# Later modulation sums and the second parts of the weight pieces on VectorE alone

## The chip, the cores and the metric

The program runs on one core of a Trainium2 chip. The metric is the device time of one execution in microseconds (us). TensorE multiplies (PE in the profile; PEld is its weight load), VectorE (DVE), ScalarE (ACT) and GpSimd (POOL) work element by element, and SyncE (SP) issues most of the loads. Each engine takes its instructions in order and waits for others by semaphores.

## The reference, cut to what matters

A network of two layers runs over 256 latent tokens of width 2048, with 256 context tokens beside them in layer 0. Everything is float32.

```python
for l in range(DEPTH):
    sh1, sc1, g1, sh2, sc2, g2 = split(silu(c) @ ada_w[l] + ada_b[l], 6)   # the modulation
    h = modulate(x_lat, norm_mix[l], sh1, sc1)
    y = even_mixer(h, hc, ...) if l % 2 == 0 else shortconv_mixer(h, ...)
    x_lat = x_lat + g1 * y
    x_lat = x_lat + g2 * swiglu(modulate(x_lat, norm_ffn[l], sh2, sc2), w_gate, w_up, w_down)
return rmsnorm(x_lat, final_norm)
```

`even_mixer` is a gated delta rule in chunks (8 heads, both directions) beside a neighbourhood attention (8 heads). The modulation is a vector times a matrix of 2048 x 12288 per layer, with nothing to reuse: its cost is the load of that matrix and one multiply-add per element.

## The kernel before, in words

**Weights.** A float32 product is made from two parts of each factor. A weight piece is 128 x 1024 numbers: `load_w` loads it (tile `raw`, 512 KB), ScalarE rounds it into `whi` (L170, called in `split_w`), and `wlo`, the rest, is `raw - whi`. For the pieces of the even mixer's input projection (112 of them, `LO_CUT = 576`) VectorE makes the first 576 columns of `wlo` (L238) and GpSimd the other 448 (L240). For all later pieces (688, `LO_CUT2 = 1024`) VectorE makes the whole. TensorE multiplies hi by hi, hi by lo and lo by hi: in `fm_stream` at L304 and L308 (256 columns a matmul), in `tm_stream` at L279, L280, L282 and, for a stream's last two steps, bank by bank at L288 to L290 (512 columns). A step of `tm_stream` over two token tiles is 12 matmuls for one piece. Pieces lie in 3 buffers of `whi` and `wlo` in the even mixer and in 4 after it; `raw` has 4 and then 6.

**The modulation.** The first sixth and second sixth of layer 0 are made on TensorE at the start (L481). All others, which the change calls the later sums, are made by `ada_job` block by block: 12 blocks of 512 columns (the even mixer and its output projection) and 14 of 1024 (layer 0's feed-forward, the odd mixer, layer 1's feed-forward). A block loads 16 tiles `araw`, one for each 128 rows, scales each by a column of `cT` and adds them up. In 12 of the 16 steps VectorE does both in one instruction, into `acc` (L335). In the steps k = 1, 5, 9, 13 ScalarE scales (L330 into `acc2` for k = 1, L332 in place for the others) and GpSimd adds into `acc2` (L333). At the end GpSimd adds `acc2` to `acc` (L337), the sum is split into `ah` and `al` (ScalarE L173, VectorE L174; blocks of 512 skip this) and TensorE adds up its partitions (L350 or L342). `araw` has 2 buffers for blocks of 1024 columns and 3 for those of 512; `acc` has one.

**What sets the order.** A `Pump` doles out steps of these blocks between the steps of the weight streams. The order on each engine is then laid out by the framework's scheduler, which models the time of every instruction. So an instruction that changes its engine or its length moves others on all engines.

**Stages in the profiled execution** (us from the start of the span): start with layer 0's first modulation to 146; the even mixer's first projections and the delta rule's matrices to 410; the rest of the even mixer, the attention and the output projection, all woven together, to 980; layer 0's feed-forward, gate and up to 1500 and down to 1755; the odd mixer to 2170; layer 1's feed-forward to the end, with modulation steps up to 2480.

Of the kernel before, what the change touches and what calls it, by code (L numbers as in the profile page):

```python
# [23 lines left out]
F32 = mybir.dt.float32  # L24
F32R = mybir.dt.float32r
AF = mybir.ActivationFunctionType
OP = mybir.AluOpType
# [5 lines left out]
FK = FH // 128  # L33
EPS = 1e-6
HD = 128
LO_CUT = 576
LO_CUT2 = 1024
RAW = 4
G2 = 4
XDT = 2  # L40
# [15 lines left out]
RAW2 = 6  # L56
SP2 = 4
# [49 lines left out]
def body(tc, x, c, ctx, c_ctx, ada_w, ada_b, norm_mix, norm_ffn, ffn_w_gate, ffn_w_up, ffn_w_down,  # L107
# [37 lines left out]
    wp = dict(pool=pool("weights", stack=wstk), raw=RAW, split=3, cut=LO_CUT)  # L145
    mm = pool("mm", bufs=4, space=PSUM)
    sm = pool("sm", bufs=2, space=PSUM)
    dram = pool("scratch", space=bass.MemoryType.DRAM)
# [79 lines left out]
            o += w  # L228
        return raw.rearrange("p k n -> p (k n)")

    def split_w(raw, cut):

        cut = wp["cut"] if cut is None else cut
        hi = wp["pool"].tile([128, 1024], F32R, name="whi", tag="whi", bufs=wp["split"])
        lo = wp["pool"].tile([128, 1024], F32R, name="wlo", tag="wlo", bufs=wp["split"])
        acopy(hi, raw)
        if cut:
            DVE.tensor_tensor(lo[:, 0:cut], raw[:, 0:cut], hi[:, 0:cut], op=OP.subtract)  # L238
        if cut < 1024:
            POOL.tensor_tensor(lo[:, cut:], raw[:, cut:], hi[:, cut:], op=OP.subtract)  # L240
        return hi, lo

    def w_steps(segs, ks, cut):

        W = sum(s[2] for s in segs)
        nk = 1024 // W
        for g in range(0, len(ks), nk):
            assert ks[g + nk - 1] == ks[g] + nk - 1
            hi, lo = split_w(load_w(segs, ks[g], nk), cut)
            for j in range(nk):  # L250
                yield ks[g] + j, hi[:, j * W:(j + 1) * W], lo[:, j * W:(j + 1) * W]

# [9 lines left out]
            else:  # L262
                yield i, []

    def tm_stream(segs, ks, lhs, toks, evac, cut=None):

        W = sum(s[2] for s in segs)
        nb = W // 512
        ps = [[None] * nb for _ in toks]
        for i, group in grouped(((k, (hi, lo) + lhs(k)) for k, hi, lo in w_steps(segs, ks, cut)), len(ks)):  # L270
            first, last = i == 0, i == len(ks) - 1
            if len(group) == 1 and not last:
                hi, lo, lh, ll = group[0]
                for ti, t in enumerate(toks):
                    a, b = lh(t), ll(t)
                    for n in range(nb):
                        if first:
                            ps[ti][n] = mmt()
                        PE.matmul(ps[ti][n], a, hi[:, n * 512:(n + 1) * 512], start=first, stop=False)  # L279
                        PE.matmul(ps[ti][n], a, lo[:, n * 512:(n + 1) * 512], start=False, stop=False)  # L280
                    for n in range(nb):
                        PE.matmul(ps[ti][n], b, hi[:, n * 512:(n + 1) * 512], start=False, stop=last)  # L282
            else:
                for ti, t in enumerate(toks):
                    for n in range(nb if group else 0):
                        for hi, lo, lh, ll in group:
                            c_ = slice(n * 512, (n + 1) * 512)
                            PE.matmul(ps[ti][n], lh(t), hi[:, c_], start=False, stop=False)  # L288
                            PE.matmul(ps[ti][n], lh(t), lo[:, c_], start=False, stop=False)  # L289
                            PE.matmul(ps[ti][n], ll(t), hi[:, c_], start=False, stop=hi is group[-1][0])  # L290
                        evac(ti, n, ps[ti][n])
            yield

    def fm_stream(segs, ks, ws, evac, cut=None):

        ps = [None] * 4
        for i, group in grouped(((k, (k, hi, lo)) for k, hi, lo in w_steps(segs, ks, cut)), len(ks)):
            for f in range(4):
                if i == 0:
                    ps[f] = mmt()  # L300
                for g, (k, hi, lo) in enumerate(group):
                    a, b = hi[:, f * 128:(f + 1) * 128], lo[:, f * 128:(f + 1) * 128]
                    if i == 0:
                        PE.matmul(ps[f][:, 0:len(ws) * 256], a, h0[:, 0:len(ws) * 256], start=True, stop=False)  # L304
                    for j, (wt, mv) in enumerate(((a, h_hi), (a, h_lo), (b, h_hi))):
                        for n, w in enumerate(ws):
                            if j or i:
                                PE.matmul(ps[f][:, n * 256:(n + 1) * 256], wt, mv(w, k), start=False,  # L308
                                          stop=i == len(ks) - 1 and g == len(group) - 1 and j == 2 and w == ws[-1])
                if i == len(ks) - 1:  # L310
                    evac(f, ps[f])
            yield


    def ada_job(pool_, l, seg, kind, gamma=None, width=1024, bufs=2):

        wr = ada_w[l].rearrange("(k p) n -> p k n", p=128)
        nf = width // 128
        for blk in range(D // width):
            c0 = seg * D + blk * width  # L320
            acc = pool_.tile([128, width], F32, name="acc", tag="acc", bufs=1)
            acc2 = pool_.tile([128, width], F32, name="acc2", tag="acc2", bufs=1)
            POOL.memset(acc, 0.0)
            SP.dma_start(acc[0:1, :], ada_b[l:l + 1, c0:c0 + width])
            for k in range(KT):
                raw = pool_.tile([128, width], F32, name="araw", tag="araw", bufs=bufs)
                SP.dma_start(raw, wr[:, k, c0:c0 + width])
                col = cT[:, k:k + 1]
                if k == 1:
                    ACT.activation(acc2, raw, AF.Copy, scale=col)  # L330
                elif k % 4 == 1:
                    ACT.activation(raw, raw, AF.Copy, scale=col)  # L332
                    POOL.tensor_tensor(acc2, raw, acc2, op=OP.add)  # L333
                else:
                    DVE.scalar_tensor_tensor(acc, raw, col, acc, op0=OP.mult, op1=OP.add)  # L335
                yield
            POOL.tensor_tensor(acc, acc, acc2, op=OP.add)  # L337
            fs_ = slice(blk * nf, (blk + 1) * nf)
            p = smt()
            if width < 1024:  # L340
                for f in range(nf):
                    PE.matmul(p[:, f:f + 1], acc[:, f * 128:(f + 1) * 128], ones[:, 0:1], start=True, stop=True)  # L342
                pc = p
            else:
                ah = pool_.tile([128, width], F32R, name="ah", tag="ah", bufs=1)
                al = pool_.tile([128, width], F32R, name="al", tag="acc2", bufs=1)
                split(ah, al, acc, DVE)
                for f in range(nf):
                    for a in (ah, al):
                        PE.matmul(p[0:nf, 0:128], pick[:, nf - 1 - f:2 * nf - 1 - f], a[:, f * 128:(f + 1) * 128],  # L350
                                  start=f == 0 and a is ah, stop=f == nf - 1 and a is al)
                g = pool_.tile([16, 128], F32, name="grow", tag="grow", bufs=1)[0:nf]
                acopy(g, p[0:nf, 0:128])
                if kind == "row":
                    ACT.dma_start(row_d[l, seg][fs_], g)
                    continue
                pc = smt()
                transpose(pc[:, 0:nf], g)
            if kind == "sc":
                DVE.scalar_tensor_tensor(scc[l, seg - 1][:, fs_], pc[:, 0:nf], 1.0, gamma[:, fs_], op0=OP.add, op1=OP.mult)  # L360
            else:
                DVE.tensor_copy((shc if kind == "sh" else gcol)[l, seg][:, fs_], pc[:, 0:nf])
        if kind == "row" and width < 1024:
            p = smt()
            transpose(p[0:16, 0:128], gcol[l, seg])
            g = pool_.tile([16, 128], F32, name="grow", tag="grow", bufs=1)
            DVE.tensor_copy(g, p[0:16, 0:128])
            SP.dma_start(row_d[l, seg], g)
# [97 lines left out]
    ks = list(range(KT))  # L466
# [667 lines left out]
    nastk.close()  # L1134
    hlstk.close()
    wstk.close()
    wp.update(pool=pool("weights2"), raw=RAW2, split=SP2, cut=LO_CUT2)
    small.append(pool("sm2", bufs=2, space=PSUM))


# [259 lines left out]
```

## Time and profile before

| | us |
|---|---|
| median of 3 runs | 2939.82 (2938.19 to 2940.96) |
| the profiled execution | 2944.36 |
| its span, first to last instruction | 2942.5 |
| TensorE busy in it | 2757.0 |
| VectorE busy | 1896.3 |
| ScalarE busy | 1335.1 |
| GpSimd busy | 587.1 |

The span is 1.9 us shorter than the execution's own time, which is 4.5 us above the median of the three timed runs. Busy time is the union of an engine's instructions; TensorE's matmuls overlap one another, so its rows give a longer time for a matmul than the distance from one to the next. The mean granted clock of TensorE is 0.981 of full speed. A measurement of this kernel can tell a difference of about 0.2% (6 us) from none.

### The profile page before, as it was taken

What the parts mean: (1) busy time and instruction counts of PE and PEld (TensorE: products, weight loads), DVE (VectorE), ACT (ScalarE), POOL (GpSimd) and SP (SyncE); (2) the same over time, 40 slices, a digit from 0 to 9 for tenths busy, and PEclk for the clock granted to TensorE, in tenths of its full rate; (3) what the DMA queues carried; (4) which work ended last, traced back from release to release, by engine and by line L of the source; (5) the groups of instructions that cost most, each with busy time, mean ns of one, the idle gap of its engine ahead of it and who ended that gap; (6) DMA issues with size and microseconds to landing.
All of it is one profiled execution on the core that took longest, in us unless ns stands there. A gap on an engine that the chain in (4) does not pass through costs nothing. (4 is left out here: it accounts for less than half of the span.)

```text
span 2942.5 us, 40694 instructions
## 1 busy us (share of the span) xinstructions
PE 2757.0 (94%) x15113; PEld 2292.6 (78%) x15113; DVE 1896.3 (64%) x2409; ACT 1335.1 (45%) x1822; POOL 587.1 (20%) x431
## 2 busy tenths in 40 slices
PE   5898998989899999999999999999999999999997
PEld 3688988878777778878877777777777888888886
DVE  3378766845566777666667867777767446445675
ACT  3245544333354444444445555453544444444554
POOL 1147535336322111110111101111101001000010
PEclk9999999999999999999999999999999999999999
DMA  9954567777767688877878766878568667656653
GB/s 344 297 156 115 159 196 242 240 225 222 218 191 245 236 290 287 301 265 260 274 252 274 261 198 239 296 259 301 196 193 294 194 186 257 187 186 217 191 193 122
DMA packets 284929, 680.80 MB, mean 231 GB/s; under 512 B 57273, under 2 KB 97313, under 8 KB 283323
## 3 DMA queue, kind: packets, MB, share of 16 engines
q1 hardware_dynamic: 262148, 652.48, 67.5%
q10 hardware_dynamic: 22583, 25.73, 2.9%
q8 instruction: 118, 1.93, 0.3%
q14 instruction: 80, 0.66, 0.1%
HBM read 657.63 MB, written 20.48 MB: 230 GB/s over the span
## 5 line engine op out<-in xcount | busy, mean ns | idle before, releaser
L238 DVE TENSOR_TENSOR wlo<-raw,whi 128x1024 fp32r<-128x1024 f32 (+1 forms) x800 | 1009.2, 1274 | 490.1 <-ACT whi L170 476.8
L170 ACT ACTIVATE whi<-raw 128x1024 fp32r<-128x1024 f32 x800 | 835.7, 1055 | 634.3 <-PE mm L282 449.5
L335 DVE SCALAR_TENSOR_TENSOR acc<-araw,cT,acc 128x1024 f32<-128x1024 f32 (+1 forms) x312 | 357.5, 1146 | 292.7 <-DMA araw<-in_ada_w_dram 252.4
L280 PE MATMUL mm<-wlo,fhi 128*128 128x512 f32 x1232 | 478.8, 394 | 3.6 <-DVE wlo L238 3.3
L279 PE MATMUL mm<-whi,fhi 128*128 128x512 f32 x1232 | 476.4, 397 | 0.0
L282 PE MATMUL mm<-whi,flo 128*128 128x512 f32 x1232 | 394.1, 393 | 0.0
L333 POOL TENSOR_TENSOR acc<-araw,acc 128x1024 f32<-128x1024 f32 (+1 forms) x78 | 155.7, 1996 | 1118.0 <-ACT araw L332 632.3
L280 PEld LDWEIGHTS mm<-wlo,fhi 128*128 128x128 f32 x1232 | 232.9, 189 | 57.8 <-DVE wlo L238 8.4
L282 PEld LDWEIGHTS mm<-whi,flo 128*128 128x128 f32 x1232 | 232.2, 189 | 50.2
L279 PEld LDWEIGHTS mm<-whi,fhi 128*128 128x128 f32 x1232 | 233.1, 189 | 48.6 <-ACT sg L1262 0.4
L279 PE MATMUL mm<-whi,ahi 128*128 128x512 f32 x672 | 262.1, 395 | 3.8 <-ACT ahi L173 2.0
L280 PE MATMUL mm<-wlo,ahi 128*128 128x512 f32 x672 | 261.8, 393 | 0.3 <-DVE wlo L238 0.3
L240 POOL TENSOR_TENSOR wlo<-raw,whi 128x448 fp32r<-128x448 f32 x112 | 160.2, 1432 | 279.8 <-ACT whi L170 259.8
L282 PE MATMUL mm<-whi,alo 128*128 128x512 f32 x672 | 211.5, 395 | 2.1 <-DVE alo L174 1.7
L332 ACT ACTIVATE araw<-araw,cT 128x1024 f32<-128x1024 f32 (+1 forms) x78 | 74.4, 954 | 301.0 <-DMA araw<-in_ada_w_dram 256.8
L308 PE MATMUL mm<-hllo,whi 128*128 128x256 f32 x640 | 184.6, 291 | 0.0
L308 PE MATMUL mm<-hlhi,wlo 128*128 128x256 f32 x600 | 172.1, 291 | 4.5 <-DVE wlo L238 4.5
L308 PE MATMUL mm<-hlhi,whi 128*128 128x256 f32 x600 | 170.2, 293 | 1.2 <-DVE hlhi L506 1.2
L1159 POOL TENSOR_TENSOR xs<-rtmp,xs 128x512 f32<-128x512 f32 x24 | 35.4, 1496 | 631.4 <-DVE rtmp L1157 631.4
L279 PEld LDWEIGHTS mm<-whi,ahi 128*128 128x128 f32 x672 | 126.8, 189 | 32.2 <-ACT ahi L173 2.8
L282 PEld LDWEIGHTS mm<-whi,alo 128*128 128x128 f32 x672 | 126.2, 189 | 32.2 <-DVE alo L174 5.1
L280 PEld LDWEIGHTS mm<-wlo,ahi 128*128 128x128 f32 x672 | 126.7, 189 | 29.4 <-DVE wlo L238 1.9
(398 smaller groups left out, 4677.6 us busy)
## 6 DMA issues: line engine op xcount, KB each, us to landing
araw<-in_ada_w_dram SPq DMA_DIRECT2D x288, 512.0 KB
raw<-in_ffn_w_down_dram SPq DMA_DIRECT2D x176, 512.0 KB
raw<-in_ffn_w_gate_dram SPq DMA_DIRECT2D x160, 512.0 KB
raw<-in_ffn_w_up_dram SPq DMA_DIRECT2D x160, 512.0 KB
raw<-in_ev_w_in_dram SPq DMA_DIRECT2D x112, 512.0 KB
araw<-in_ada_w_dram SPq DMA_DIRECT2D x192, 256.0 KB
raw<-in_od_w_in_dram SPq DMA_DIRECT2D x96, 512.0 KB
raw<-in_ev_w_out_dram SPq DMA_DIRECT2D x32, 512.0 KB
```

The costliest lines, as they stand in the source:

```text
L170: ACT.activation(dst, src, AF.Copy)
L238: DVE.tensor_tensor(lo[:, 0:cut], raw[:, 0:cut], hi[:, 0:cut], op=OP.subtract)
L240: POOL.tensor_tensor(lo[:, cut:], raw[:, cut:], hi[:, cut:], op=OP.subtract)
L279: PE.matmul(ps[ti][n], a, hi[:, n * 512:(n + 1) * 512], start=first, stop=False)
L280: PE.matmul(ps[ti][n], a, lo[:, n * 512:(n + 1) * 512], start=False, stop=False)
L282: PE.matmul(ps[ti][n], b, hi[:, n * 512:(n + 1) * 512], start=False, stop=last)
L308: PE.matmul(ps[f][:, n * 256:(n + 1) * 256], wt, mv(w, k), start=False, stop=i == len(ks) - 1 and g == len(group) - 1 and j == 2 and w == ...
L332: ACT.activation(raw, raw, AF.Copy, scale=col)
L333: POOL.tensor_tensor(acc2, raw, acc2, op=OP.add)
L335: DVE.scalar_tensor_tensor(acc, raw, col, acc, op0=OP.mult, op1=OP.add)
L1159: eng.tensor_tensor(v, tmp, v, op=OP.add)
```

## The change

The second part of a weight piece is always made by VectorE in one instruction of 1024 columns; the cuts are gone. In the modulation all 16 steps of a block are VectorE's multiply-add; ScalarE's scaling, GpSimd's adds and the final add are gone, and so is the tile `acc2`, whose place `al` had shared. GpSimd keeps its other work (zeroing `acc`, the delta rule's helpers, the residual adds).

```diff
@@ split_w
         acopy(hi, raw)
-        if cut:
-            DVE.tensor_tensor(lo[:, 0:cut], raw[:, 0:cut], hi[:, 0:cut], op=OP.subtract)
-        if cut < 1024:
-            POOL.tensor_tensor(lo[:, cut:], raw[:, cut:], hi[:, cut:], op=OP.subtract)
+        DVE.tensor_tensor(lo, raw, hi, op=OP.subtract)
         return hi, lo
@@ ada_job
             acc = pool_.tile([128, width], F32, name="acc", tag="acc", bufs=1)
-            acc2 = pool_.tile([128, width], F32, name="acc2", tag="acc2", bufs=1)
             POOL.memset(acc, 0.0)
...
                 SP.dma_start(raw, wr[:, k, c0:c0 + width])
-                col = cT[:, k:k + 1]
-                if k == 1:
-                    ACT.activation(acc2, raw, AF.Copy, scale=col)
-                elif k % 4 == 1:
-                    ACT.activation(raw, raw, AF.Copy, scale=col)
-                    POOL.tensor_tensor(acc2, raw, acc2, op=OP.add)
-                else:
-                    DVE.scalar_tensor_tensor(acc, raw, col, acc, op0=OP.mult, op1=OP.add)
+                DVE.scalar_tensor_tensor(acc, raw, cT[:, k:k + 1], acc, op0=OP.mult, op1=OP.add)
                 yield
-            POOL.tensor_tensor(acc, acc, acc2, op=OP.add)
...
-                al = pool_.tile([128, width], F32R, name="al", tag="acc2", bufs=1)
+                al = pool_.tile([128, width], F32R, name="al", tag="al", bufs=1)
```

In the changed program the lines have other numbers: the multiply-add is L321 (was L335), `wlo` L234 (was L238), `whi` L168 (was L170), the split of a sum L171 and L172 (were L173 and L174), the evacuations of layer 0's up stream L1251 (was L1266) and of the odd mixer L1309 (was L1324).

The order moves on every engine. Three places carry the prediction. The first is VectorE in layer 0's feed-forward, up to the evacuation `sg` of the second up stream; before, from the split `al` of a modulation block on:

```order
L174 TENSOR_TENSOR al<-acc,ah 128x1024
L238 TENSOR_TENSOR wlo<-raw,whi 128x1024
L335 SCALAR_TENSOR_TENSOR acc<-araw,cT,acc 128x1024
L238 TENSOR_TENSOR wlo<-raw,whi 128x1024 x3
L335 SCALAR_TENSOR_TENSOR acc<-araw,cT,acc 128x1024
L238 TENSOR_TENSOR wlo<-raw,whi 128x1024 x2
L335 SCALAR_TENSOR_TENSOR acc<-araw,cT,acc 128x1024
L238 TENSOR_TENSOR wlo<-raw,whi 128x1024 x2
L335 SCALAR_TENSOR_TENSOR acc<-araw,cT,acc 128x1024
L238 TENSOR_TENSOR wlo<-raw,whi 128x1024 x6
L1266 TENSOR_TENSOR sg<-mm,sg 128x512 x4
```

The same place of the changed program, up to the same evacuation:

```order
L234 TENSOR_TENSOR wlo<-raw,whi 128x1024 x2
L321 SCALAR_TENSOR_TENSOR acc<-araw,cT,acc 128x1024
L234 TENSOR_TENSOR wlo<-raw,whi 128x1024
L321 SCALAR_TENSOR_TENSOR acc<-araw,cT,acc 128x1024
L234 TENSOR_TENSOR wlo<-raw,whi 128x1024
L321 SCALAR_TENSOR_TENSOR acc<-araw,cT,acc 128x1024
L234 TENSOR_TENSOR wlo<-raw,whi 128x1024
L321 SCALAR_TENSOR_TENSOR acc<-araw,cT,acc 128x1024
L234 TENSOR_TENSOR wlo<-raw,whi 128x1024 x2
L321 SCALAR_TENSOR_TENSOR acc<-araw,cT,acc 128x1024
L234 TENSOR_TENSOR wlo<-raw,whi 128x1024
L1251 TENSOR_TENSOR sg<-mm,sg 128x512 x4
```

The multiply-adds stand closer together. Counted in the orders from a block's first multiply-add to its last, the 14 blocks of 1024 columns hold 15 to 19 weight pieces each in the changed program; before, six held 16 to 20 (layer 0's first two, three of the odd mixer's four and layer 1's first) and the other eight 25 to 31, one 70.

The second place is ScalarE there. Before, around the evacuation `sg` of a gate stream:

```order
L170 ACTIVATE whi<-raw 128x1024 x5
L332 ACTIVATE araw<-araw,cT 128x1024
L170 ACTIVATE whi<-raw 128x1024 x6
L332 ACTIVATE araw<-araw,cT 128x1024
L1262 ACTIVATE sg<-mm 128x512 x3
L170 ACTIVATE whi<-raw 128x1024
L1262 ACTIVATE sg<-mm 128x512
L170 ACTIVATE whi<-raw 128x1024 x3
L173 ACTIVATE ah<-acc 128x1024
```

And in the changed program:

```order
L168 ACTIVATE whi<-raw 128x1024 x7
L171 ACTIVATE ah<-acc 128x1024
L168 ACTIVATE whi<-raw 128x1024 x5
L1247 ACTIVATE sg<-mm 128x512 x3
L168 ACTIVATE whi<-raw 128x1024
L1247 ACTIVATE sg<-mm 128x512
L168 ACTIVATE whi<-raw 128x1024 x17
```

The scalings between the `whi` are gone, and with them the places where ScalarE could wait for an `araw` to land.

The third place is VectorE at the end of the odd mixer's first value stream, where `u_t` takes the sums out of PSUM. Before:

```order
L335 SCALAR_TENSOR_TENSOR acc<-araw,cT,acc 128x1024
L238 TENSOR_TENSOR wlo<-raw,whi 128x1024
L1324 TENSOR_TENSOR u_t<-mm,u_t 128x512 x4
L335 SCALAR_TENSOR_TENSOR acc<-araw,cT,acc 128x1024
L238 TENSOR_TENSOR wlo<-raw,whi 128x1024 x2
```

In the changed program:

```order
L321 SCALAR_TENSOR_TENSOR acc<-araw,cT,acc 128x1024
L234 TENSOR_TENSOR wlo<-raw,whi 128x1024
L1309 TENSOR_TENSOR u_t<-mm,u_t 128x512
L321 SCALAR_TENSOR_TENSOR acc<-araw,cT,acc 128x1024
L1309 TENSOR_TENSOR u_t<-mm,u_t 128x512 x2
L321 SCALAR_TENSOR_TENSOR acc<-araw,cT,acc 128x1024
L1309 TENSOR_TENSOR u_t<-mm,u_t 128x512
L234 TENSOR_TENSOR wlo<-raw,whi 128x1024 x2
```

Two multiply-adds now stand among the four evacuations. Over all streams from layer 0's feed-forward on six stand so, and one did before.

More of the change, by code (lines that the diff above doesn't have):

```diff
@@ L144, in body @@
     wstk = Stack()
-    wp = dict(pool=pool("weights", stack=wstk), raw=RAW, split=3, cut=LO_CUT)
+    wp = dict(pool=pool("weights", stack=wstk), raw=RAW, split=3)
     mm = pool("mm", bufs=4, space=PSUM)
@@ L229, in load_w, with split_w @@
         return raw.rearrange("p k n -> p (k n)")
-    def split_w(raw, cut):
-        cut = wp["cut"] if cut is None else cut
+    def split_w(raw):
         hi = wp["pool"].tile([128, 1024], F32R, name="whi", tag="whi", bufs=wp["split"])
@@ L263, in grouped, with tm_stream @@
                 yield i, []
[L265 removed]
+    def tm_stream(segs, ks, lhs, toks, evac):
         W = sum(s[2] for s in segs)
@@ L269, in tm_stream @@
         ps = [[None] * nb for _ in toks]
-        for i, group in grouped(((k, (hi, lo) + lhs(k)) for k, hi, lo in w_steps(segs, ks, cut)), len(ks)):
+        for i, group in grouped(((k, (hi, lo) + lhs(k)) for k, hi, lo in w_steps(segs, ks)), len(ks)):
             first, last = i == 0, i == len(ks) - 1
@@ L292, in tm_stream, with fm_stream @@
             yield
-    def fm_stream(segs, ks, ws, evac, cut=None):
+    def fm_stream(segs, ks, ws, evac):
         ps = [None] * 4
-        for i, group in grouped(((k, (k, hi, lo)) for k, hi, lo in w_steps(segs, ks, cut)), len(ks)):
+        for i, group in grouped(((k, (k, hi, lo)) for k, hi, lo in w_steps(segs, ks)), len(ks)):
             for f in range(4):
@@ L1136, in body @@
     wstk.close()
-    wp.update(pool=pool("weights2"), raw=RAW2, split=SP2, cut=LO_CUT2)
+    wp.update(pool=pool("weights2"), raw=RAW2, split=SP2)
     small.append(pool("sm2", bufs=2, space=PSUM))
```

6 lines of the change are left out of this document (2 added, 4 removed).

## The prediction

> **What bounds the kernel now.** I read the page first: busy time by engine.
>
> ```profile
> PE 2757.0 (94%) x15113; PEld 2292.6 (78%) x15113; DVE 1896.3 (64%) x2409; ACT 1335.1 (45%) x1822; POOL 587.1 (20%) x431
> ```
>
> TensorE sets the end. Its matmuls are the same before and after, so the change can only move TensorE's idle time. The windows view, cut at the stages, says where that is (window, its length, then busy us of PE, PEld, DVE, ACT, POOL, granted clock, DMA share, GB/s):
>
> ```profile
> 146.00:410.00 264.00, 243.29 (x1941) 239.31 (x1941) 211.94 (x364) 131.33 (x196) 142.60 (x136) 0.96 0.48 142
> 410.00:980.00 570.00, 517.61 (x3973) 448.04 (x3972) 356.47 (x593) 229.51 (x407) 221.67 (x181) 0.98 0.74 230
> 980.00:1500.00 520.00, 509.18 (x2308) 415.06 (x2309) 357.34 (x325) 245.94 (x277) 64.64 (x29) 0.99 0.79 274
> 1500.00:1755.00 255.00, 242.55 (x1066) 192.94 (x1066) 183.96 (x206) 134.62 (x195) 35.10 (x15) 0.99 0.73 245
> 1755.00:2170.00 415.00, 389.36 (x1748) 313.62 (x1746) 299.77 (x338) 191.25 (x245) 58.50 (x30) 0.98 0.74 251
> 2170.00:2480.00 310.00, 300.87 (x1339) 246.27 (x1340) 189.08 (x193) 143.01 (x164) 22.91 (x10) 0.98 0.70 229
> ```
>
> Length less PE busy is idle time: 20.7 and 52.4 us in the even mixer's two stages, 10.8, 12.5, 25.6 and 9.1 in the four with blocks of 1024 columns. Before 146 and after 2480 the change touches little. So at most 131 us are in play, and the table of waits says for whom TensorE waits. First from 980 to 2480 (us in total, times, longest):
>
> ```profile
> PE sm L189 <- DVE xc L1174: 18.3, 3, 6.3
> PE sm L189 <- DVE sg L1266: 7.3, 2, 4.4
> PE mm L279 <- DVE u_t L1324: 7.2, 2, 4.3
> PE mm L280 <- DVE wlo L238: 5.4, 10, 1.0
> PE sm L189 <- DVE sg L1278: 4.9, 1, 4.9
> PE mm L289 <- DVE wlo L238: 2.8, 4, 1.0
> PE mm L279 <- ACT ahi L173: 2.0, 2, 1.0
> PE mm L282 <- DVE alo L174: 1.7, 4, 0.6
> PE mm L290 <- DVE alo L174: 1.4, 1, 1.4
> ```
>
> Three kinds: the norms between layers (xc, 18.3, untouched), late second parts and splits (5.4 + 2.8 + 2.0 + 1.7 + 1.4 = 13.3), and evacuations at a stream's end that VectorE made late (7.3 + 7.2 + 4.9 = 19.4). In the even mixer, from the table for the whole run, those that name GpSimd, and the longest one of VectorE's and ScalarE's convolution chain:
>
> ```profile
> PE sm L189 <- ACT cv L562: 12.6, 8, 2.8
> ...
> PE sm L1092 <- POOL bq L1087: 2.7, 1, 2.7
> ...
> PE gd L772 <- POOL gm L768: 2.5, 4, 0.8
> ...
> PE gd L883 <- POOL acc L333: 2.3, 1, 2.3
> ...
> PE sm L342 <- POOL acc L337: 1.6, 2, 0.9
> ```
>
> **The change part by part: VectorE's load.** How long its instructions take undisturbed, from the timeline (start, us):
>
> ```profile
> 602.67 0.75 DVE L335 SCALAR_TENSOR_TENSOR acc<-araw,cT,acc 128x512 f32<-128x512 f32 x1 [3.42 <-DMA araw<-in_ada_w_dram]
> 603.34 0.75 DVE L238 TENSOR_TENSOR wlo<-raw,whi 128x576 fp32r<-128x576 f32 x1
> 1871.79 1.22 DVE L238 TENSOR_TENSOR wlo<-raw,whi 128x1024 fp32r<-128x1024 f32 x1
> 1872.93 1.28 DVE L335 SCALAR_TENSOR_TENSOR acc<-araw,cT,acc 128x1024 f32<-128x1024 f32 x1
> ```
>
> Added: 112 whole pieces in place of 576 columns, 112 x (1.22 - 0.75) = 53 us; 4 steps in each of 14 wide and 12 narrow blocks, 56 x 1.28 + 48 x 0.75 = 108 us. Together 161 us. Against it stands what GpSimd costs VectorE today. The group means are well above those times:
>
> ```profile
> L238 DVE TENSOR_TENSOR wlo<-raw,whi 128x1024 fp32r<-128x1024 f32 x688 | 892.7, 1311 | 398.7 <-ACT whi L170 394.4 <-DMA raw<-in_ffn_w_up_dram 2.8
> L335 DVE SCALAR_TENSOR_TENSOR acc<-araw,cT,acc 128x1024 f32<-128x1024 f32 x168 | 227.5, 1354 | 180.4 <-DMA araw<-in_ada_w_dram 160.9 <-DMA acc<-in_ada_b_dram 10.3 <-issue 8.7
> L335 DVE SCALAR_TENSOR_TENSOR acc<-araw,cT,acc 128x512 f32<-128x512 f32 x144 | 130.0, 903 | 112.3 <-DMA araw<-in_ada_w_dram 91.5 <-DMA acc<-in_ada_b_dram 8.9 <-issue 8.0
> L238 DVE TENSOR_TENSOR wlo<-raw,whi 128x576 fp32r<-128x576 f32 x112 | 116.5, 1042 | 91.5 <-ACT whi L170 82.4 <-issue 5.2 <-DMA nd<-n 3.6
> ```
>
> The excess is 688 x 0.09 + 168 x 0.07 + 144 x 0.15 + 112 x 0.29 = 62 + 12 + 22 + 32 = 128 us. One case in the timeline shows its cause, a piece of 1024 columns that starts in the middle of a GpSimd add and ends 1.1 us after it, 2.58 us in place of 1.22:
>
> ```profile
> 1203.44 2.41 POOL L333 TENSOR_TENSOR acc<-araw,acc 128x1024 f32<-128x1024 f32 x1 [15.23 <-ACT araw L332]
> 1204.34 2.58 DVE L238 TENSOR_TENSOR wlo<-raw,whi 128x1024 fp32r<-128x1024 f32 x1 [1.75 <-ACT whi L170]
> ```
>
> Most of this excess goes, since the GpSimd work that goes is 160.2 + 155.7 + 64.7 = 381 of its 587 us:
>
> ```profile
> L240 POOL TENSOR_TENSOR wlo<-raw,whi 128x448 fp32r<-128x448 f32 x112 | 160.2, 1432 | 279.8 <-ACT whi L170 259.8 <-DMA qTd<-qf 5.9 <-issue 4.8
> L333 POOL TENSOR_TENSOR acc<-araw,acc 128x1024 f32<-128x1024 f32 (+1 forms) x78 | 155.7, 1996 | 1118.0 <-ACT araw L332 632.3 <-ACT acc L330 466.8 <-DVE sg L1266 11.9
> L337 POOL TENSOR_TENSOR acc<-acc,acc 128x1024 f32<-128x1024 f32 (+1 forms) x26 | 64.7, 2490 | 118.0 <-issue 108.7 <-DVE acc L335 3.4 <-DMA raw<-in_ev_w_out_dram 2.8
> ```
>
> So VectorE's busy time stays within some 30 to 50 us of what it was: about 1930 to 1945 us. The Trainium skill, page SBUF — State Buffer, section Who interferes with whom, has a VectorE instruction with two inputs in SBUF and a reading GpSimd instruction shut each other out for a whole instruction; by that rule up to GpSimd's full 381 us could come back, while the rows show 128.
>
> **ScalarE and the loads.** ScalarE loses its scalings, and two kinds of wait in which it held up the `whi` queued behind (waits of ScalarE, then of VectorE):
>
> ```profile
> ACT araw L332 <- DMA araw<-in_ada_w_dram: 256.8, 62, 9.4
> ...
> ACT ah L173 <- POOL acc L337: 77.4, 14, 7.3
> ...
> ACT acc L330 <- POOL acc L337: 22.4, 6, 6.2
> ```
>
> ```profile
> DVE acc L335 <- DMA araw<-in_ada_w_dram: 252.4, 156, 5.1
> ```
>
> The second and third go. The first moves: 104 more multiply-adds wait for `araw` on VectorE. At its mean, 252.4 / 312 = 0.81 us, that is 84 us of blocking where ScalarE had 257; behind a blocked VectorE stand the `wlo` and evacuations that TensorE needs, covered by the pieces made ahead. SP's 416 loads of `araw` stay and stand closer together. GpSimd's queue keeps zeroing `acc`; the chain between blocks loses L337.
>
> **The sum**, made against the profiled execution of 2944.4 us (span 2942.5 and 1.9 around it), which lies 4.5 us above the median; I take the differences to the median. (a) Late second parts and splits, 13.3 us: the stretched pieces go, the closer multiply-adds bring some back; -3, between -13 (all gone) and +13 (as much again). (b) Six multiply-adds among the evacuations where one was: one costs at most 1.28 + 0.81 = 2.1 us of lateness, and half is hidden behind the other banks' last matmuls; +5, between 0 and +11. (c) The even mixer: the waits for L333 and L337 go (3.9), half of those for `bq` and `gm` (2.6), since GpSimd's queue before them empties, and a third of the convolution's 12.6 (my estimate; its multiply-adds meet L240 today); -10, between -25 (a third of the 73 us idle there) and +13 (as much again as the convolution waits, if longer pieces on VectorE delay the small steps). Sum -8: **2932 us**.
>
> **The rivals.** *Slower: the closer blocks outrun the loads.* A wide block is now 16 loads of `araw` and about 17 of weights, 33 x 0.524 MB in the time TensorE takes for 17 pieces of 12 matmuls. Two matmuls in the chain of work that ended last (start, us):
>
> ```profile
> 2107.72 0.46 PE mm L282 x2
> ```
>
> So a piece is 2.75 us, and 17.3 MB in 46.8 us would be 370 GB/s. The page's rates by slice:
>
> ```profile
> GB/s 344 297 156 115 159 196 242 240 225 222 218 191 245 236 290 287 301 265 260 274 252 274 261 198 239 296 259 301 196 193 294 194 186 257 187 186 217 191 193 122
> ```
>
> No slice went above 344, and 301 after the start. VectorE would stand at an `araw` while `wlo` and evacuations wait; the three pieces ahead (8.2 us) cover rates down to 17.3 MB in 55 us, 315 GB/s, and below that it decides. Its price is to be read from blocks that were as close before: the odd mixer's 25.6 us less its norm (6.1) over four blocks is 4.9 each, gate and up of layer 0 have (10.8 - 6.1) / 6 = 0.8. Seven blocks that were wide apart become close: 7 x 4.1 = 29, and with (c) 2940 + 29 - 10 = 2959 us. Against it: the gaps between blocks become longer, so the lead comes back.
>
> *No change.* VectorE's sum is near zero, TensorE is 94% busy, and what ScalarE no longer waits for VectorE does: 2940 us.
>
> *Slower: whole pieces come late for their first columns.* In the even mixer a piece's first 512 columns serve one step and the others the next; the first are ready after 0.75 us today and after 1.22 then. All exposed that is 53 us, a quarter 13: 2953 us. Against it: the split's second half takes GpSimd 1.43 us (L240), longer than the whole. The Trainium skill, page Perfetto Trace Analysis, section Optimizing Scalar/DVE Operations, advises breaking instructions up where an unsaturated engine makes others wait; by that rule this is the outcome, and L240's row speaks against it here.
>
> **How the numbers follow.** Forecast 0.44, close blocks 0.29, no change 0.22, late columns 0.05. A measurement tells 0.2% (5.9 us) from none, so faster 0.44, same 0.22, slower 0.34. The forecast's own range is 2908 (all of (c)) to 2934; the range of 8 in 10 takes in no change and most of the close blocks: 2908 to 2962.
>
> **What would show it.** Right: no L240, L333, L337; group means of `wlo` near 1.22 and of the multiply-add near 1.28 and 0.75; VectorE busy 1915 to 1960; ScalarE without L330 and L332; fewer waits of TensorE for GpSimd in 410 to 980. Wrong: more idle TensorE between 980 and 2480 than 58 us, with VectorE waiting for `araw` much over 340 us in all (the first rival); or idle time in the even mixer grown by VectorE's names.

## The result, and the profile after

The changed kernel takes 2881.91 us (median of 5 runs, 2877.6 to 2893.09), the kernel before beside it 2938.19 (5 runs, 2933.56 to 2940.96): a ratio of 0.9823, with an interval of 0.9804 to 0.9842. It is 1.8% faster, and faster than the lower end of the predicted range. The profiled execution took 2891.65 us (span 2889.6), 9.7 above its median; the one before took 2944.36.

From the page of the changed kernel: the span, the busy time by engine, and the rates by slice.

```profile
span 2889.6 us, 40293 instructions
...
PE 2747.0 (95%) x15113; PEld 2297.8 (80%) x15113; DVE 1896.9 (66%) x2513; ACT 1263.6 (44%) x1720; POOL 216.0 (7%) x215
...
GB/s 342 300 171 133 145 205 252 242 216 193 221 176 224 215 336 318 330 266 273 308 277 265 230 190 239 336 310 298 178 206 327 241 182 183 190 188 216 192 191 123
```

VectorE's busy time is what it was (1896.3 before), though it has 104 instructions more. GpSimd lost 371 us of work. The windows, cut at the same stages (window, length, busy us of PE, PEld, DVE, ACT, POOL, granted clock, DMA share, GB/s):

```profile
146.00:410.00 264.00, 249.50 (x2048) 246.29 (x2046) 204.61 (x373) 134.44 (x196) 79.08 (x88) 0.99 0.53 155
410.00:987.00 577.00, 521.52 (x3889) 451.27 (x3889) 362.29 (x632) 201.22 (x359) 81.76 (x79) 0.94 0.72 222
987.00:1497.00 510.00, 504.21 (x2305) 413.90 (x2306) 373.98 (x362) 225.24 (x255) 6.68 (x7) 0.99 0.83 293
1497.00:1746.00 249.00, 248.04 (x1119) 201.99 (x1117) 177.13 (x211) 136.84 (x195) 9.26 (x8) 1.00 0.71 233
1746.00:2125.00 379.00, 371.39 (x1698) 304.06 (x1698) 289.41 (x342) 170.41 (x219) 12.75 (x12) 0.99 0.79 269
2125.00:2430.00 305.00, 299.60 (x1349) 246.43 (x1349) 190.47 (x202) 136.97 (x159) 2.62 (x3) 0.99 0.72 235
```

The four stages with wide blocks (the last four rows) last 1443 us where they lasted 1500. TensorE's idle time in them (length less busy) is 5.8, 1.0, 7.6 and 5.4 us, 19.8 in all, where it was 58.0. Its busy time fell too, from 1442.0 to 1423.2, with the same matmuls: the granted clock reads 0.99, 1.00, 0.99, 0.99 where it read 0.99, 0.99, 0.98, 0.98. So 38 of the 57 us are idle time that went, and 19 are busy time, of which the clock accounts for a part. The even mixer (the first two rows) gave nothing back. What TensorE waits for in the four stages now, the longest of the table of waits (us, times, longest):

```profile
PE sm L187 <- DVE xc L1159: 18.0, 3, 6.4
PE mm L273 <- ACT u_t L168: 1.2, 1, 1.2
PE mm L274 <- DVE wlo L234: 1.0, 1, 1.0
PE mm L273 <- DVE u_t L1309: 0.3, 1, 0.3
```

The norms between layers are left. The late second parts and splits (13.3 us before) are down to 1.0, the late evacuations by VectorE (19.4) to 0.3. VectorE's groups, with shapes apart:

```profile
L234 DVE TENSOR_TENSOR wlo<-raw,whi 128x1024 fp32r<-128x1024 f32 x800 | 982.9, 1235 | 494.0 <-ACT whi L168 484.7 <-DMA araw<-in_ada_w_dram 6.9 <-PE mm L302 0.8
L321 DVE SCALAR_TENSOR_TENSOR acc<-araw,cT,acc 128x1024 f32<-128x1024 f32 x224 | 287.4, 1283 | 123.4 <-DMA araw<-in_ada_w_dram 115.1 <-DMA acc<-in_ada_b_dram 3.6 <-issue 1.5
L321 DVE SCALAR_TENSOR_TENSOR acc<-araw,cT,acc 128x512 f32<-128x512 f32 x192 | 149.8, 780 | 120.6 <-DMA araw<-in_ada_w_dram 107.3 <-DMA acc<-in_ada_b_dram 11.2
L172 DVE TENSOR_TENSOR alo<-prodT,ahi 128x256 fp32r<-128x256 f32 x176 | 79.5, 454 | 67.8 <-PE mm L276 62.8 <-ACT ahi L171 5.0
```

The means, 1.235, 1.283 and 0.780 us, are close to the undisturbed 1.22, 1.28 and 0.75. The second row holds the surprise. 224 wide multiply-adds wait 115.1 us for `araw`, 0.51 each; before, 168 of them waited 160.9, 0.96 each. And ScalarE had the wait of its own that is gone, in the same stages of the kernel before:

```profile
ACT araw L332 <- DMA araw<-in_ada_w_dram: 155.1, 35, 9.4
```

What such a wait did is seen at the end of layer 0's last gate-and-up stream, in the kernel before. First VectorE's timeline (start, us, instruction, idle time before it), then the add of GpSimd that ran at its start and the issue of the next two loads:

```profile
1494.98 3.51 DVE L335 SCALAR_TENSOR_TENSOR acc<-araw,cT,acc 128x1024 f32<-128x1024 f32 x1 [1.07 <-DMA araw<-in_ada_w_dram]
1498.41 2.35 DVE L238 TENSOR_TENSOR wlo<-raw,whi 128x1024 fp32r<-128x1024 f32 x2
1504.50 1.28 DVE L335 SCALAR_TENSOR_TENSOR acc<-araw,cT,acc 128x1024 f32<-128x1024 f32 x1 [3.74 <-DMA araw<-in_ada_w_dram]
1505.70 1.28 DVE L1278 TENSOR_TENSOR sg<-mm,sg 128x512 f32<-128x512 f32 x2
```

```profile
1494.99 2.41 POOL L333 TENSOR_TENSOR acc<-araw,acc 128x1024 f32<-128x1024 f32 x1 [14.83 <-ACT araw L332]
...
1498.51 0.89 SPq L327 DMA_DIRECT2D araw<-in_ada_w_dram  x2
```

A multiply-add stretched to 3.51 us beside GpSimd's add holds its buffer until 1498.49; at 1498.51 the next two loads are issued. The next multiply-add then stands 3.74 us for its load, and the evacuations `sg` stand behind it. The changed kernel in the same stage:

```profile
1496.43 1.27 DVE L321 SCALAR_TENSOR_TENSOR acc<-araw,cT,acc 128x1024 f32<-128x1024 f32 x1
1497.63 0.68 DVE L1263 TENSOR_TENSOR sg<-mm,sg 128x512 f32<-128x512 f32 x1
1498.65 1.29 DVE L321 SCALAR_TENSOR_TENSOR acc<-araw,cT,acc 128x1024 f32<-128x1024 f32 x1 [0.34 <-DMA araw<-in_ada_w_dram]
1499.85 0.68 DVE L1263 TENSOR_TENSOR sg<-mm,sg 128x512 f32<-128x512 f32 x1
```

One multiply-add stands just ahead of the evacuations and one between them; the first does not wait, the second waits 0.34 us.

### The profile page after: what moved, and what is told of

Read it like the earlier page. It is cut to its first block, busy times and chain, and to the rows that moved or that the text cites. A ratio compares the mean times of both kernels' runs of the same rounds, so it can differ in the third digit from the quotient of the medians.

```text
span 2889.6 us, 40293 instructions
## 1 busy us (share of the span) xinstructions
PE 2747.0 (95%) x15113; PEld 2297.8 (80%) x15113; DVE 1896.9 (66%) x2513; ACT 1263.6 (44%) x1720; POOL 216.0 (7%) x215
## 4 chain that ended last, share of the span: by engine, by line
PE 74%; DMA 12%; DVE 7%; issue 2%; ACT 2%; POOL 1%; SPq 1%; ACTq 0%; DVEq 0%; POOLq 0%
PE mm L273 19%; PE mm L274 19%; PE mm L276 19%; DMA araw<-in_ada_w_dram 7%; PE mm L302 6%; DVE wlo L234 2%; PE mm L282 2%; PE sm L187 2%; PE mm L284 2%; PE mm L283 2%; DVE acc L321 2%; DMA br<-in_ev_rpb_dram 1%; PE gd L466 1%; DMA acc<-in_ada_b_dram 1%; DMA kb_d<-nst 0%
## 5 line engine op out<-in xcount | busy, mean ns | idle before, releaser
L234 DVE TENSOR_TENSOR wlo<-raw,whi 128x1024 fp32r<-128x1024 f32 x800 | 982.9, 1235 | 494.0 <-ACT whi L168 484.7
L168 ACT ACTIVATE whi<-raw 128x1024 fp32r<-128x1024 f32 x800 | 842.4, 1059 | 926.4 <-PE mm L276 668.4
L321 DVE SCALAR_TENSOR_TENSOR acc<-araw,cT,acc 128x1024 f32<-128x1024 f32 (+1 forms) x416 | 437.2, 1051 | 244.0 <-DMA araw<-in_ada_w_dram 222.4
L171 ACT ACTIVATE ahi<-prodT 128x256 fp32r<-128x256 f32 x176 | 73.2, 417 | 193.7 <-PE mm L274 186.5
L274 PE MATMUL mm<-wlo,dhi 128*128 128x512 f32 x336 | 128.3, 395 | 0.0
L302 PEld LDWEIGHTS mm<-hllo,whi 128*128 128x128 f32 x640 | 127.9, 200 | 0.6
L273 PE MATMUL mm<-whi,dhi 128*128 128x512 f32 x336 | 126.7, 397 | 1.5 <-ACT u_t L168 1.2
```

What stands on the lines that cost most here:

```text
L168: ACT.activation(dst, src, AF.Copy)
L171: ACT.activation(hi, src, AF.Copy)
L234: DVE.tensor_tensor(lo, raw, hi, op=OP.subtract)
L321: DVE.scalar_tensor_tensor(acc, raw, cT[:, k:k + 1], acc, op0=OP.mult, op1=OP.add)
```

## The experiments

**The theory** that came out of this: `araw` has two buffers, and a load is issued only when its buffer is free. A shared step held its buffer through ScalarE's scaling and GpSimd's add, and GpSimd's adds stretched VectorE's steps, so that those held theirs longer. Later loads were issued late, and VectorE and ScalarE, which go in order, stood at an `araw` with `wlo`, `whi` and evacuations behind. **Rivals**: GpSimd's adds alone, by stretching what TensorE needs (no buffers in it); ScalarE's queue alone; the whole weight pieces; the narrow sums of the even mixer.

Each ratio is to the kernel before, run beside the one that is measured. "After the first norm" is the time from the first `xc` (983.9 us before, 991.2 in the changed kernel) to the span's end in the profiled execution: 1958.6 us before, 1898.4 changed. It comes from one execution of each kernel, so a few us of it are scatter.

**Which part of the change.** The sums alone (pieces as before), the pieces alone, and the wide blocks' sums alone:

e1, the kernel before with the loop of the changed one (the pieces stay cut at 576):

```diff
...
-                if k == 1:
-                    ACT.activation(acc2, raw, AF.Copy, scale=col)
-                elif k % 4 == 1:
-                    ACT.activation(raw, raw, AF.Copy, scale=col)
-                    POOL.tensor_tensor(acc2, raw, acc2, op=OP.add)
-                else:
-                    DVE.scalar_tensor_tensor(acc, raw, col, acc, op0=OP.mult, op1=OP.add)
+                DVE.scalar_tensor_tensor(acc, raw, cT[:, k:k + 1], acc, op0=OP.mult, op1=OP.add)
                 yield
-            POOL.tensor_tensor(acc, acc, acc2, op=OP.add)
```

> Kernel before with all modulation steps on VectorE, the second parts still cut at 576 for the even mixer. Theory A (the gain is the modulation's): 2880 to 2895 us. Rival B (the whole second parts carry half of it): about 2910 us.

e2, the kernel before with whole pieces:

```diff
-LO_CUT = 576
+LO_CUT = 1024
```

> Kernel before with whole second parts on VectorE everywhere, the modulation still shared with ScalarE and GpSimd. Theory A: no gain beyond the even mixer, 2930 to 2950 us. Rival B: about 2910 us.

e3, the kernel before with the wide blocks' sums on VectorE alone:

```diff
...
-                if k == 1:
+                if width == 1024 or k % 4 != 1:
+                    DVE.scalar_tensor_tensor(acc, raw, col, acc, op0=OP.mult, op1=OP.add)
+                elif k == 1:
...
-            POOL.tensor_tensor(acc, acc, acc2, op=OP.add)
+            if width < 1024:
+                POOL.tensor_tensor(acc, acc, acc2, op=OP.add)
```

> Kernel before with only the 14 blocks of 1024 columns on VectorE alone; the narrow blocks and the second parts as before. Theory A in its narrow form (all of the gain lies after the even mixer, which itself lost some us by the change): 2870 to 2885 us, at or below the changed kernel, with the stage from 990 us to the end about 60 us shorter than before. Rival (the even mixer's new order gives part of it): above 2900 us.

Measured: e1 2893.08 us (ratio 0.9851, 0.9824 to 0.9878), e3 2888.51 (0.984, 0.9814 to 0.9866), both near the changed kernel; e2 2953.43 (1.0049, 1.0032 to 1.0067), slower. After the first norm e1 takes 1904.5, e3 1904.6, e2 1953.2. So within the scatter (1898.4 to 1904.6 us) the whole gain lies in the 14 wide blocks. The whole pieces by themselves cost 0.5%; the first norm begins at 999.4 us in e2. The windows row of its even mixer: VectorE is no busier there (356.39 us against 356.47), while TensorE idles 590 - 514.34 = 75.7 us, where it idled 52.4.

```profile
410.00:1000.00 590.00, 514.34 (x3890) 444.80 (x3890) 356.39 (x598) 229.78 (x408) 146.34 (x123) 0.95 0.70 218
```

What grew there was not settled. With the narrow sums moved as well, nothing of it is left: over six kernels with both (the changed one, e4, e6, e9, e11, e13) the first norm begins at 972 to 991 us, mean 980; over eight with neither at 978 to 985, mean 982.

**GpSimd's adds on top of the changed kernel.** e4 adds what GpSimd did in a wide block without using the result: its adds read `araw` as it landed, and so hold its buffer. e6 holds the buffer with writes only.

e4, with an `acc2` of its own, zeroed at the block's start:

```diff
...
                 DVE.scalar_tensor_tensor(acc, raw, cT[:, k:k + 1], acc, op0=OP.mult, op1=OP.add)
+                if width == 1024 and k in (5, 9, 13):
+                    POOL.tensor_tensor(acc2, raw, acc2, op=OP.add)
                 yield
+            if width == 1024:
+                POOL.tensor_tensor(acc2, acc, acc2, op=OP.add)
```

> Changed kernel, plus GpSimd adds of 128 x 1024 that nothing uses, in steps 5, 9 and 13 of each wide block and at its end, reading the same tiles as before; VectorE's and ScalarE's work is that of the changed kernel. Theory port (VectorE loses its time to GpSimd's reads): the means of VectorE's wide instructions rise again by 0.06 to 0.1 us and half or more of the gain goes, 2910 to 2935 us. Rival queue (ScalarE's waits for loads and for GpSimd were what held up the pieces): within 10 us of the changed kernel, 2880 to 2892 us.

e6:

```diff
                 DVE.scalar_tensor_tensor(acc, raw, cT[:, k:k + 1], acc, op0=OP.mult, op1=OP.add)
+                if width == 1024 and k in (5, 9, 13):
+                    POOL.memset(raw, 0.0)
+                    POOL.memset(raw, 1.0)
```

> Changed kernel, plus two GpSimd fills of the araw tile after VectorE has read it, in steps 5, 9 and 13 of each wide block: the buffer comes free about 1.9 us later, as an add of GpSimd holds it in the kernel before, but GpSimd reads nothing. Theory port: within 12 us of the changed kernel, up to 2895 us, VectorE's means unchanged (1.235 and 1.283 us). Rival buffers (the add's cost is that araw comes free late, so the next load and VectorE's wait for it): 2915 us or more.

Measured: e4 2964.42 us (1.0085, 1.0053 to 1.0117): the whole gain is lost, and more, which is beyond both expectations; after the first norm 1968.9, in an execution of 2942.98 that was its shortest. e6 2909.42 (0.9914, 0.9882 to 0.9946), between the two expected ranges; 1914.3, 16 us over the changed kernel. VectorE's groups in e4, then in e6:

```profile
L324 DVE SCALAR_TENSOR_TENSOR acc<-araw,cT,acc 128x1024 f32<-128x1024 f32 x224 | 376.0, 1679 | 102.7 <-DMA araw<-in_ada_w_dram 89.4 <-DMA acc<-in_ada_b_dram 5.7 <-issue 5.0
```

```profile
L321 DVE SCALAR_TENSOR_TENSOR acc<-araw,cT,acc 128x1024 f32<-128x1024 f32 x224 | 287.4, 1283 | 179.5 <-DMA araw<-in_ada_w_dram 165.0 <-DMA acc<-in_ada_b_dram 9.0 <-issue 4.3
```

In e6 no step is stretched (1283 as in the changed kernel), and the wait for `araw` rises from 115.1 to 165.0 us: holding alone costs. VectorE's order is nearly that of the changed kernel (61 of its 1380 instructions after the first norm stand otherwise). In e4 the steps are stretched to 1679 ns, and TensorE waits for VectorE's parts again:

```profile
PE mm L274 <- DVE wlo L234: 24.0, 22, 2.7
...
PE mm L273 <- DVE u_t L1316: 8.3, 2, 6.4
PE sm L187 <- DVE sg L1258: 7.1, 3, 3.9
```

The stretch in e4's timeline, GpSimd's row and then VectorE's: a multiply-add that starts together with the add ends 1.1 us after it.

```profile
1101.84 2.40 POOL L326 TENSOR_TENSOR acc<-araw,acc 128x1024 f32<-128x1024 f32 x1 [11.49 <-DMA araw<-in_ada_w_dram]
...
1101.80 3.53 DVE L324 SCALAR_TENSOR_TENSOR acc<-araw,cT,acc 128x1024 f32<-128x1024 f32 x1
```

The Trainium skill, page SBUF — State Buffer, section Who interferes with whom, has a VectorE instruction with two inputs in SBUF contend with a GpSimd instruction that reads SBUF and not with one that only writes: e4 and e6 agree with both halves (1679 against 1283 ns).

**One part of the old sharing at a time**, from the kernel before: in e5 ScalarE scales but VectorE adds, in e7 GpSimd adds unscaled data (the scaling of steps 5, 9 and 13 is left out, and step 1 is a multiply-add), in e8 only the last add, L337, goes to VectorE.

e5:

```diff
-                    POOL.tensor_tensor(acc2, raw, acc2, op=OP.add)
+                    (DVE if width == 1024 else POOL).tensor_tensor(acc2, raw, acc2, op=OP.add)
...
-            POOL.tensor_tensor(acc, acc, acc2, op=OP.add)
+            (DVE if width == 1024 else POOL).tensor_tensor(acc, acc, acc2, op=OP.add)
```

> Kernel before, but in the wide blocks the adds of GpSimd (into acc2 and at the end) are VectorE's plain adds; ScalarE scales as before and still waits for its loads between the whi. No GpSimd instruction reads SBUF there but the residual's. Theory port: the gain stays, 2885 to 2900 us. Rival queue (ScalarE's scalings and their waits hold up the pieces): 2925 us or more.

e7:

```diff
+                if width == 1024 and k == 1:
+                    POOL.memset(acc2, 0.0)
+                    DVE.scalar_tensor_tensor(acc, raw, col, acc, op0=OP.mult, op1=OP.add)
...
-                    ACT.activation(raw, raw, AF.Copy, scale=col)
+                    if width < 1024:
+                        ACT.activation(raw, raw, AF.Copy, scale=col)
                     POOL.tensor_tensor(acc2, raw, acc2, op=OP.add)
```

> Kernel before with ScalarE out of the wide blocks: GpSimd adds the tiles of steps 5, 9 and 13 unscaled (the scaling by cT of these three steps is left out), VectorE does step 1, GpSimd still makes the last add. Theory port: the time stays near the kernel before, 2920 to 2945 us. Rival queue: 2885 to 2900 us.

e8:

```diff
-            POOL.tensor_tensor(acc, acc, acc2, op=OP.add)
+            (DVE if width == 1024 else POOL).tensor_tensor(acc, acc, acc2, op=OP.add)
```

> Kernel before with only the last add of a wide block (14 of its 56 GpSimd adds, and the one that ScalarE's ah waits for, 77 us in all) on VectorE. Theory port, by the number of adds: a quarter of the gain, 2920 to 2930 us. Rival (ScalarE's wait for that add is what delays the pieces): half of the gain or more, 2910 us or less.

Measured: e5 2903.58 us (0.9891, 0.9859 to 0.9923), e7 2917.97 (0.994, 0.992 to 0.996), e8 2930.45 (0.9982, 0.9964 to 1.0); after the first norm 1919.8, 1932.7 and 1949.1. So without GpSimd the shared steps still cost 21 us (e5), and without the scalings GpSimd's adds cost 34 (e7), both against the changed kernel; against e3, whose pieces and narrow sums are the same as theirs, it is 15 and 28. L337 is worth some 10 at most, and its interval ends at 1.0, no difference. Neither rival alone holds the whole. e5's waits for `araw`, on VectorE in the same stages, were 139.6 us, and ScalarE waited 143.9 (138.9 of them for L332).

**The stretch without the hold.** In e9 GpSimd's adds work on a tile of their own, so that they stretch VectorE's steps but touch no `araw`:

```diff
...
                 DVE.scalar_tensor_tensor(acc, raw, cT[:, k:k + 1], acc, op0=OP.mult, op1=OP.add)
+                if width == 1024 and k in (5, 9, 13, 15):
+                    POOL.tensor_copy(acc2[:, 0:16], acc[:, 0:16])
+                    POOL.tensor_tensor(acc2, acc2, acc2, op=OP.add)
```

> Changed kernel, plus GpSimd adds of 128 x 1024 on a tile of its own, each set off by a copy of 16 columns of acc after steps 5, 9, 13 and 15 of a wide block: the reads of the adds are there, but no araw is held. Theory port: from the first norm to the end 1935 to 1960 us where the changed kernel has 1898, the multiply-add's mean well over 1.283 us or the wlo's over 1.235. Theory buffers (an add costs by holding araw, as the fills did with +16): within 8 us of 1898.

Measured: 2918.81 us (0.9941, 0.9917 to 0.9964); 1932.4 after the first norm, 34 over the changed kernel; the multiply-adds last 1476 ns. So the stretch has a price without any longer hold by another engine. VectorE's wide multiply-adds wait less for `araw` here than in the changed kernel (92.2 us against 115.1; e4: 89.4), so this price does not show as a longer wait for loads.

**One more buffer.** Five kernels get a third `araw` buffer in the wide blocks (the narrow ones have three already, by `AB`): the kernel before (e10), the changed one (e11), e3 (e12), e9 (e13) and e5 (e14).

```diff
-                raw = pool_.tile([128, width], F32, name="araw", tag="araw", bufs=bufs)
+                raw = pool_.tile([128, width], F32, name="araw", tag="araw", bufs=3)
```

> Kernel before with three araw buffers in the wide blocks in place of two, nothing else. If a held buffer is a part of what the old way cost: 10 to 20 us less after the first norm (1959 before), VectorE waiting less than 161 us for araw. If only the port and ScalarE's queue cost: within 5 us of 1959.

> Changed kernel with three araw buffers in the wide blocks. TensorE's waits left after the first norm are 18 us of norms and 3 us of others, so little can be won: 0 to 5 us under the changed kernel's 1898 after the first norm, although VectorE's waits for araw (115 us there) fall.

> The kernel with only the wide blocks on VectorE alone, and three araw buffers in them: the even mixer of the kernel before with the best of the rest. If the even mixer really lost a few us by the change, this is the fastest, 2870 to 2880 us; if that was the scatter of one profiled execution, it stands level with the changed kernel, 2880 to 2890 us.

> Changed kernel with the GpSimd adds that hold nothing (steps 5, 9, 13 and 15 of each wide block) and three araw buffers. Theory direct (the lock at the port costs by VectorE's longer instructions themselves): 25 to 40 us over the 1892 us that the changed kernel with three buffers needs after the first norm. Theory through the buffers (longer instructions free araw late, and two buffers pass this on to the loads): within 12 us of 1892, with the instructions' means still stretched.

> Kernel before with VectorE's plain adds in place of GpSimd's in the wide blocks, ScalarE scaling, and three araw buffers. If ScalarE's scalings cost by holding up the whi: 10 to 20 us over 1892 after the first norm, as with two buffers they were 15 over the changed kernel's. If they too cost through the two buffers: within 6 us of 1892.

Measured, in us (times are medians; each ratio is to the kernel before that ran beside it, at 2933.89 to 2938.19 us):

| kernel | two buffers: time | after the first norm | three buffers: time (ratio, interval) | after the first norm |
|---|---|---|---|---|
| before | 2938.19 | 1958.6 | 2901.03 (0.9875, 0.9846 to 0.9905) | 1915.9 |
| ScalarE scales, VectorE adds | 2903.58 | 1919.8 | 2880.98 (0.9812, 0.9788 to 0.9836) | 1897.6 |
| changed, GpSimd's own adds | 2918.81 | 1932.4 | 2880.37 (0.9819, 0.9785 to 0.9854) | 1896.2 |
| wide sums alone | 2888.51 | 1904.6 | 2873.86 (0.9783, 0.975 to 0.9817) | 1892.4 |
| changed | 2881.91 | 1898.4 | 2869.99 (0.9776, 0.9742 to 0.981) | 1891.9 |

With the third buffer the kernel before gains 43 us after the first norm, of the change's 60 and more than twice what was expected. Its steps are stretched as much as ever, and TensorE hardly minds. No other line of the program differs, but the scheduler lays the order out anew: of VectorE's 1324 instructions after the first norm 98 stand out of the old order (counted in the traces), as many as the change itself moves. So the 43 us are the buffer and the order that came with it; a run of the old order with three buffers is missing. e10's two groups of VectorE, and then its waits of TensorE in those stages:

```profile
L238 DVE TENSOR_TENSOR wlo<-raw,whi 128x1024 fp32r<-128x1024 f32 x688 | 897.7, 1315 | 439.9 <-ACT whi L170 436.9 <-DMA raw<-in_ffn_w_up_dram 1.2
L335 DVE SCALAR_TENSOR_TENSOR acc<-araw,cT,acc 128x1024 f32<-128x1024 f32 x168 | 226.2, 1346 | 88.6 <-DMA araw<-in_ada_w_dram 86.1 <-DMA acc<-in_ada_b_dram 1.2 <-issue 0.4
```

```profile
PE mm L280 <- DVE wlo L238: 5.4, 6, 1.5
PE mm L279 <- ACT ahi L173: 2.6, 3, 1.2
...
PE sm L189 <- DVE sg L1278: 1.5, 1, 1.5
```

The means are the old ones (1315 and 1346), the wait for `araw` is 86.1 in place of 160.9, and the late evacuations, 19.4 us before, are one of 1.5 and one of 0.7. e13 is the counterpart of e9: its multiply-adds are stretched even more, and cost 4 us after the first norm where they had cost 34 (by the medians of the whole time, 10 where they had cost 37). Here the orders are nearly the same: 19 of VectorE's 1380 instructions stand otherwise in e13 than in e11, and 35 otherwise in e9 than in the changed kernel.

```profile
L324 DVE SCALAR_TENSOR_TENSOR acc<-araw,cT,acc 128x1024 f32<-128x1024 f32 x224 | 352.2, 1572 | 27.6 <-DMA araw<-in_ada_w_dram 15.0 <-DMA acc<-in_ada_b_dram 8.9 <-POOL acc L326 0.4
```

e14 points the same way for ScalarE's scalings: 6 us in place of 21 (against e12 and e3, 5 in place of 15), though its order moved more (118 of 1380, from e5). So the stretch has most of its price only while there are two buffers, and holding one has a price of its own (e6). That a stretched step costs because it frees its buffer late is argued from this and not shown: VectorE without waits for loads may as well have the time to make a stretch good. The lowest median is that of the changed kernel with three buffers, whose wide multiply-adds wait 12.4 us for `araw` in all; e12 (2867.04 to 2878.73 us) cannot be told from it (2869.15 to 2873.59).

```profile
L321 DVE SCALAR_TENSOR_TENSOR acc<-araw,cT,acc 128x1024 f32<-128x1024 f32 x224 | 286.6, 1280 | 18.3 <-DMA araw<-in_ada_w_dram 12.4 <-DMA acc<-in_ada_b_dram 4.3
```

Left open as well: with three buffers the kernel before is still 24 us behind the changed one after the first norm, and adds (4) and scalings (6) do not make that up one by one. Both together still make VectorE wait 86.1 us for `araw`; whether a fourth buffer would take that was not tried.

## Why the prediction was wrong, point by point

- **VectorE's load**: right in kind. 161 us were added, and GpSimd's stretch went. Nearly all 161 came back, and not 128: some 108 from the four groups (1420.1 us against 1366.7, with 161 added) and the rest from smaller steps that the sum left out (`alo` went from 520 to 454 ns, 91.3 to 79.5 us), so busy time is 1896.9 and not 1930 to 1945. Busy time was never what decided.
- **The step that failed** is "The first moves: 104 more multiply-adds wait for `araw` on VectorE. At its mean, 252.4 / 312 = 0.81 us, that is 84 us of blocking". It takes the wait for a load as a property of the load. It was a property of the buffers: two of them, held by stretched steps and by two more engines. With those gone, 416 multiply-adds wait less than 312 did (222.4 us against 252.4), and in the wide blocks 115.1 against 160.9 with 56 more of them; where fills hold the buffers again (e6) it is 165.0, and with a third buffer (e11) 12.4. In the sum the step stands in term (b): the 0.81 us in its price, and its lower bound of 0, which takes the 19.4 us of late evacuations as staying.
- **Terms (a) and (b)** inherit it. (a), late second parts and splits, came to about -12 (13.3 to 1.0) and not -3: that was inside its bounds. (b) was taken at +5, between 0 and +11, and came to about -19 (19.4 to 0.3): six multiply-adds among the evacuations do no harm when they hardly wait, and the 19.4 us that I left standing came from waits for `araw`. The rows at 1504 show one of the five cases; the other four (at 1082, 1876, 2027 and 2274 us of the profile before) follow within 6 us on a multiply-add that had stood 1.5 to 4.4 us for its load. The bound excluded a gain without a reason.
- **Not in the sum at all**: TensorE's busy time, 19 us less, against "the change can only move TensorE's idle time". The mean granted clock rose from 0.985 to 0.992 over the four stages (weighted by their lengths), about 9 us of 1442. That fewer stalls cause it was not tested, and the other 10 have no row that names them.
- **(c), the even mixer**: -10 was taken, nothing is measured, and that may be two effects that cancel. The waits for GpSimd went, others came (11.1 us for a transfer, 7.9 for `nst` by ScalarE), and the first norm begins at the same time within the scatter. But the granted clock from 410 to 970 us reads 0.93 to 0.95 in the six profiles with both moves and 0.96 to 0.98 in the eight with neither (from 146 to 410 it is 0.98 to 0.99 against 0.96 to 0.97), so a lower clock may hide a gain. Why it is lower was not tested. The two longest new waits:

```profile
PE gd L868 <- DMA xd<-dz: 11.1, 4, 6.5
PE mm L298 <- ACT nst L1038: 7.9, 1, 7.9
```

- **The first rival**, closer blocks that outrun the loads, was given 0.29. It fell at its own point: it decides below 315 GB/s, and the first three full slices of layer 0's gate and up now show 336, 318 and 330, while TensorE idles 5.8 us in that stage. Its price of 4.1 us a block was read from blocks whose stalls are mostly gone with three buffers in the kernel before (e10), and it was counted for seven blocks where eight came closer.
- **No change** (0.22) argued that TensorE is 94% busy and VectorE's sum near zero. Both hold, and 56 us went all the same: most of it is idle time that waits at the head of a queue had made, and VectorE's busy time does not tell of these.
- **The range**: its low end, 2908, is called all of (c), but the terms with (c) at -25 give 2940 - 3 + 5 - 25 = 2917, and with all three at their lower ends 2902. The measured 2881.91 lies below each.
- **Late first columns** (0.05): whole pieces alone are 15 us slower (e2), near that rival's 2953, and in the stage that it named; beside the moved sums nothing of it remains. The Trainium skill's advice to break instructions up (Perfetto Trace Analysis, Optimizing Scalar/DVE Operations) is borne out by e2's time if by anything here, but no row of e2 shows that columns were late, and by e1 and the changed kernel whole pieces make no difference once the sums have moved.

## What to carry to other kernels

A mean wait for a load is no price to carry over to more such waits: here it was 0.96 us before, 0.51 after the change and 0.06 with a third buffer. Ask first how long each buffer is held, by every engine that touches it, and how many there are. Before work is moved off an engine that waits for loads, try one more buffer; here that, with the order that came with it, gave 43 of 60 us, and with the change on top 67. Equal busy sums (1896.3 and 1896.9 us) said nothing of the time here, where engines go in order and a wait at the head of a queue holds up what stands behind.

## What the runs showed of the hardware

- A multiply-add on VectorE that starts together with GpSimd's add of 128x1024 lasts 3.53 us, the add's 2.40 and 1.1 of its own (1.28 undisturbed), while writes alone by GpSimd leave it at 1283 ns in the mean (e6).
- 66 us of such stretch over 224 steps (352.2 against 286.6 us, e13 and e11) cost 4 us after the first norm with three buffers (10 by the medians), and 43 us of it (330.7 against 287.4, e9 and the changed kernel) cost 34 with two (37).
- The DMA engines moved 336 GB/s in a slice of 72 us in the middle of the changed kernel, with TensorE 95% busy over the span; in the kernel before, no slice after the start went above 301.
